# Soft mixture of experts on one core: weights of the next stage fetched in steps from float16 copies, transposed x kept in DRAM, a plain first block, and PSUM seeded by ScalarE

## The chip, the cores and the metric

The kernel runs on one core of one Trainium2 chip. The metric is the device time of one execution in microseconds; the kernel before takes 1645.31 us (median of three executions).

## The reference

Every token goes through all eight experts, and the results are summed with softmax weights of its eight router logits:

```python
probs = softmax(router_logits)                      # (16, 512, 8)
for e in range(8):                                  # x: (16, 512, 512)
    output += probs[:, :, e:e+1] * (x @ expert_weights[e])   # weights: (8, 512, 2048)
```

So it is one product of an 8192 x 4096 matrix (x scaled by each expert's probability, experts side by side) with a 4096 x 2048 matrix, all of it float32 outside the kernel. The kernel multiplies in float16 and accumulates in float32.

## The kernel before

The rows are cut into 32 blocks `h` of 256 (`HQ`), the inner dimension into the first four and the last four experts, the output columns into two halves of 1024. A Strassen-like scheme with seven products instead of eight runs over these halves, where even blocks `h` are the upper and odd ones the lower half of the rows. Four of the seven products are computed by `sub_product`, which splits each once more in the same way (seven products of 8 matmuls in place of eight). The other three are plain and belong to the last loop.

The program has five stages, and this text calls them A, B, C, D and main:

- A: `sub_product(0, P1, ...)`, the first four experts with the left columns. Its results go to DRAM (`kept[1]`).
- B: `sub_product(0, P2, ...)`, the last four experts with the left columns. It loads A's results (`from_kept(1, ...)`), adds them to its products on VectorE (`keep` with `v`), and writes a finished quarter of the output.
- C: `sub_product(1, PQ, ...)`, with differences of weights, into `kept[5]`.
- D: `sub_product(1, P2, ...)`, with other differences, into `kept[4]`.
- main: 16 pairs of blocks, two 128-row halves `u` each: 32 rounds. A round has six products of 16 matmuls (`s2` with `w6`, `s3` with `w7`, `s4` with `w3`, two column blocks each), adds `kept` 1, 4 and 5 on VectorE, and stores three quarters of the output.

In `sub_product` a step `d` takes two blocks `h`: it loads x and the probabilities, makes the seven scaled operands `z` (eight VectorE instructions of 128x2048 float16 for the products with the probabilities and for sums and differences), and runs 2 x 56 matmuls of 128x512. There are eight steps in a stage.

x is loaded anew in each stage: `load_x` casts 128 rows from float32 to float16 by a DMA on the GpSimd queue (line 101), then transposes them by a DMA on SyncE's queue (line 102). The probabilities are written once to DRAM (`p_dram`) and broadcast over the partitions by `load_p` (line 107).

Weights are tiles of 128 x 8 x 512 float16 (1 MB): two experts by 512 columns. `load_w` fills one with two casting DMAs on the GpSimd queue (line 122), 1 MB of float32 read by each. There are 12 such tiles in `wpool`. A stage uses seven: four quarters, of which one is overwritten in place, and three more that `inner_weights` makes by VectorE subtractions (`t1`, `t2`, `t4`). C's four quarters need four subtractions more and D's need twelve; eight tiles of D's intermediate results are stored to DRAM (`td`, line 236) and loaded in main as `w6` and `w7` (line 244). `w3` is cast from float32 again.

All VectorE additions go through the helper `tt` (line 69), all matmuls through `mm` (line 143). PSUM has eight banks of 128x512. Every engine and each DMA queue runs its instructions in an order that is written out when the program is built: a planner plays the program through, and it gives each engine the earliest instruction in program order that is ready by its own reckoning and for which a buffer is free. On the chip each engine then follows that order and waits at an instruction whose inputs are late, with all that stands behind it.

## Time and profile before

| | |
|---|---|
| three executions | 1644.45, 1645.31 and 1648.5 us; median 1645.31 us |
| the profiled execution | 1647.06 us, of which the span is 1645.3 us |
| TensorE matmuls | 1465.4 us busy (89%), 6656 matmuls |
| VectorE | 1070.4 us busy (65%), 1126 instructions |
| ScalarE | 115.2 us (7%) |
| GpSimd | 156.1 us (9%), 268 instructions, nearly all of them the issue of DMAs |
| HBM | 235.14 MB read, 126.03 MB written |
| mean granted TensorE clock | 0.958 of full |

Durations in the rows below come from the one profiled execution. A matmul's own duration overlaps with that of its neighbours, so how fast TensorE goes is read from the number of matmuls in a stretch. "Idle before, releaser" is how long the engine stood still ahead of an instruction, and what ended this.

### The profile page before, as it was taken

To read this page: it belongs to the slowest core of one execution; us is meant where nothing else is said; L and a number is where in the kernel's file an instruction comes from. 1 tells how busy PE (TensorE), PEld (TensorE's weight loads), DVE (VectorE), ACT (ScalarE), POOL (GpSimd) and SP (SyncE) were. 2 spreads that over 40 slices of the span, in tenths; PEclk is the share of its full clock that TensorE was granted. 3 is DMA by queue.
4 is the path that set the end of the run, shared out by engine and by line. 5 is a ranking of instruction groups with operands and counts; after the bars stand their busy time and mean duration, and the time that the engine had idled before them with its cause. 6 is when DMAs were issued, how large, how long until landed. Compare 5 with 4: busy or idle time off the path is not lost.

```text
span 1645.3 us, 17059 instructions
## 1 busy us (share of the span) xinstructions
PE 1465.4 (89%) x6656; PEld 656.7 (40%) x6656; DVE 1070.4 (65%) x1126; ACT 115.2 (7%) x196; POOL 156.1 (9%) x268
## 2 busy tenths in 40 slices
PE   1799993679999564899999979999999999999998
PEld 0344441234443221344444433444444444444444
DVE  3775672488876344856665657877777777777733
ACT  0111110000001010111111100000000000000000
POOL 2211020101011211000000010000000000000000
PEclk9899998889999787899999988999999999999999
DMA  9998669989899999668865499766676666665432
GB/s 177 182 230 186 148 149 243 218 208 227 220 209 231 265 236 184 161 148 219 224 149 150 136 272 246 223 200 208 201 205 204 206 202 205 202 204 195 165 150 104
DMA packets 243409, 324.58 MB, mean 197 GB/s; under 512 B 118272, under 2 KB 179712, under 8 KB 241280
## 3 DMA queue, kind: packets, MB, share of 16 engines
q1 hardware_dynamic: 177664, 260.56, 52.5%
q0 software_dynamic: 65664, 62.93, 25.4%
q8 instruction: 52, 0.85, 0.2%
q14 instruction: 29, 0.24, 0.1%
HBM read 235.14 MB, written 126.03 MB: 220 GB/s over the span
## 4 chain that ended last, share of the span: by engine, by line
PE 66%; DMA 9%; issue 2%; DVE 1%; POOL 0%; SPq 0%; ACT 0%; DVEq 0%; POOLq 0%; ACTq 0%
PE ps L143 66%; DMA w<-in_expert_weights_dram 5%; DMA xs<-in_x_dram 1%; DMA t<-w 1%; DMA xT<-xs 1%; DVE w L69 1%; POOL w L122 0%; DVE z L69 0%; DVE m L69 0%; SPq L102 0%; ACT r L183 0%; SPq L107 0%; SPq L202 0%; DVEq L69 0%; SPq L236 0%
## 5 line engine op out<-in xcount | busy, mean ns | idle before, releaser
L143 PE MATMUL ps<-w,z 128*128 128x512 f16 x6656 | 1465.4, 384 | 175.4 <-DVE z L69 77.6
L143 PEld LDWEIGHTS <-z 128*128 128x128 f16 x6656 | 656.7, 99 | 983.6 <-issue 136.5
L69 DVE TENSOR_TENSOR z<-xT,pT 128x2048 f16<-128x2048 f16 x256 | 308.8, 1218 | 28.4 <-DMA xT<-xs 13.4
L69 DVE TENSOR_TENSOR z<-z 128x2048 f16<-128x2048 f16 x224 | 272.6, 1219 | 18.5 <-PE ps L143 16.6
L69 DVE TENSOR_TENSOR m<-ps,m 128x512 f32<-128x512 f32 x192 | 130.6, 689 | 198.9 <-PE ps L143 190.3
L69 DVE TENSOR_TENSOR m<-ps,r 128x512 f32<-128x512 f32 x192 | 131.6, 687 | 134.4 <-PE ps L143 101.8
L101 POOL DMA_DIRECT2D xs<-in_x_dram x192 | 102.2, 534 | 1180.5 <-DMA xT<-xs 1161.3
L69 DVE TENSOR_TENSOR w<-w 128x4096 f16<-128x4096 f16 x32 | 73.1, 2288 | 151.1 <-DMA w<-in_expert_weights_dram 108.5
L183 ACT COPY r<-ps 128x512 f32<-128x512 f32 x192 | 112.6, 586 | 825.7 <-PE ps L143 726.4
L69 DVE TENSOR_TENSOR m<-m 128x1024 f32<-128x1024 f32 x96 | 114.4, 1219 | 0.3
L122 POOL DMA_DIRECT2D w<-in_expert_weights_dram x72 | 54.0, 760 | 145.7 <-DVE w L69 83.9
L69 DVE TENSOR_TENSOR r<-ps,m 128x512 f32<-128x512 f32 x64 | 43.6, 687 | 22.0 <-PE ps L143 16.9
L69 DVE TENSOR_TENSOR m<-r,ps 128x512 f32<-128x512 f32 x64 | 43.7, 682 | 9.8 <-PE ps L143 9.7
L80 DVE TENSOR_REDUCE mx<-lg 128x64 f32<-128x512 f32 x1 | 0.7, 686 | 6.9 <-DMA lg<-in_router_logits_dram 6.9
L82 ACT ACT_TABLE_LOAD x1 | 1.3, 1283 | 6.9 <-DMA lg<-in_router_logits_dram 6.9
L84 DVE TENSOR_REDUCE sm<-lg 128x64 f32<-128x512 f32 x1 | 0.7, 686 | 0.7 <-ACT lg L82 0.7
L89 ACT CAST ph<-pf 128x256 f16<-128x256 f32 x1 | 0.4, 404 | 10.0 <-DVE pf L69 10.0
L69 DVE TENSOR_TENSOR pf<-lg,sm 128x512 f32<-128x512 f32 x1 | 1.1, 1065 | 0.0
L69 DVE TENSOR_TENSOR lg<-lg,mx 128x512 f32<-128x512 f32 x1 | 0.7, 693 | 0.0
L82 ACT ACTIVATE lg<-lg 128x512 f32<-128x512 f32 x1 | 0.6, 630 | 0.2 <-DVE lg L69 0.2
L85 DVE RECIPROCAL sm<-sm 128x64 f32<-128x64 f32 x1 | 0.6, 553 | 0.0
L69 DVE TENSOR_TENSOR ph<-pf 128x256 f16<-128x256 f32 x1 | 0.4, 426 | 0.0
(5 smaller groups left out, 0.8 us busy)
## 6 DMA issues: line engine op xcount, KB each, us to landing
m<-kept SPq DMA_DIRECT2D x128, 512.0 KB, 5.3
out_dram<-m SPq DMA_DIRECT2D x128, 512.0 KB, 3.6
kept<-m SPq DMA_DIRECT2D x96, 512.0 KB, 4.1
w<-in_expert_weights_dram POOLq DMA_DIRECT2D x72, 512.0 KB, 13.5
pT<-p_dram SPq DMA_DIRECT2D x128, 256.0 KB, 4.4
xs<-in_x_dram POOLq DMA_DIRECT2D x192, 128.0 KB, 5.3
t<-w SPq DMA_DIRECT2D x8, 1024.0 KB, 7.6
w<-t SPq DMA_DIRECT2D x8, 1024.0 KB, 6.7
```

What stands on the lines that cost most here:

```text
L69: nc.vector.tensor_tensor(out=o, in0=a, in1=b, op=op)
L80: nc.vector.tensor_reduce(out=mx, in_=lg, axis=AX, op=mybir.AluOpType.max)
L82: nc.scalar.activation(out=lg, in_=lg, func=mybir.ActivationFunctionType.Exp)
L84: nc.vector.tensor_reduce(out=sm, in_=lg, axis=AX, op=ADD)
L85: nc.vector.reciprocal(out=sm, in_=sm)
L89: nc.scalar.copy(ph[:, 0:HE], pf[:, HE:E])
L101: nc.gpsimd.dma_start(out=xs, in_=x_f[ds(h * HQ + j * P, P), :])
L122: nc.gpsimd.dma_start(out=t[:, ds(e * C, C), :], in_=expert_weights[e0 + e, :, ds(n0, NB)].rearrange("(c p) n -> p c n", p=P))
L143: nc.tensor.matmul(ps, z, w, start=start, stop=stop, skip_group_check=True)
L183: nc.scalar.copy(r, ps)
```

## The change

- Weights: each 512-column block that is cast from float32 is stored once as float16 in DRAM (`raw`) by a DMA on the GpSimd queue; later uses load that copy (1 MB, one DMA, also GpSimd). Two sets of differences are stored likewise (`t1d`, `t2d`). The fetching, subtracting and storing for the next stage is a generator (`prep`) of which one step is taken in the program after each step `d` of the running stage.
- x: the first time that a block is used, `load_x` casts and transposes it and stores the result in DRAM (`x_dram`); later uses load this by one DMA on SyncE's queue.
- Start: step `d = 0` of stage A is computed plainly: 512 rows, 128 matmuls in place of 112, with operands that TensorE makes (16 matmuls of x by a diagonal matrix of probabilities, which transposes and scales at once; the results are copied out by ScalarE and VectorE). The 512 rows have a small softmax of their own. Eight matmuls of zeros open the eight PSUM banks.
- Stage B stores its results (`kept[2]`) and adds nothing; its evictions are copies on ScalarE as in the other stages. Main loads `kept[2]`, adds it to `kept[1]` on VectorE (128x1024) and stores that quarter of the output.
- main: ScalarE copies `kept[1]` into two PSUM banks, the products with `w6` accumulate on this, and the products with `w7` accumulate on the same two banks after VectorE has read them. Three VectorE additions of 128x1024 in a round are gone, one new one is there, and two more evictions of 128x512.
- Buffers: `xpool` 8 tiles in place of 9, `spool` 5 in place of 3.

The core of the diff:

```diff
+    with tc.tile_pool(name="psum0", bufs=1, space=bass.MemoryType.PSUM) as psum0:
+        ...
+        for i in range(8):
+            nc.tensor.matmul(every[:, i, :], zero[:, 0:P], zero, start=True, stop=True)
...
+    def fetch(q, k, n, keep=True):
+        t = new_w()
+        if (q, k, n) in raw:
+            nc.gpsimd.dma_start(out=t, in_=raw[q, k, n])
+        else:
+            cast_w(q, k, n, t)
+            if keep:
+                save(raw, (q, k, n), t)
+        return t
+    def save(where, key, t):
+        where[key] = dram.tile([P, K8, NB], f16, name="wd" + "_".join(map(str, key)))
+        nc.gpsimd.dma_start(out=where[key], in_=t)
...
+    for j in range(NF):
+        diag = rpool.tile([P, HE, P], f16, name="diag", tag="r")
+        tt(diag, ident..., ph0..., MUL)
+        for c in range(C):
+            ps = bank()
+            mm(ps, xs0[j][:, ds(c * P, P)], diag.rearrange("p e t -> p (e t)"), True, True)
+            (nc.scalar.copy if c % 2 else nc.vector.tensor_copy)(z[:, :, c, :], ps...)
...
+        if h in x_dram:
+            nc.sync.dma_start(out=xT, in_=x_dram[h])
+        else:
+            ... (cast and transpose as before)
+            nc.sync.dma_start(out=x_dram[h], in_=xT)
...
+    def sub_product(r, odd, first, w, prep, start=0, xs=None):
+        steps = prep()
+        for d in range(start, NI // 2):
...
+            next(steps, None)
...
+    def weights_of_t1():                       # made during B, for C
+        for kn in BLOCKS:
+            t = fetch(22, *kn)
+            if kn[0] == 1:
+                yield
+        b = {}
+        for kn in BLOCKS:
+            t = fetch(12, *kn)
+            b[kn] = fetch(11, *kn)
+            tt(b[kn], t, b[kn], SUB)
+            save(t1d, kn, b[kn])
+            yield
+        ready[5] = yield from inner_weights(b)
+    def weights_of_t4():                       # made during C, for D
+        for kn in BLOCKS:
+            t, t2 = fetch(22, *kn), load(t1d, kn)
+            tt(t2, t, t2, SUB)
+            save(t2d, kn, t2)
+            b[kn] = fetch(21, *kn)
+            tt(b[kn], t2, b[kn], SUB)
+            yield
+    def weights_of_main():                     # made during D
+        for kn in BLOCKS:
+            t = fetch(22, *kn)
+            w7[kn] = fetch(12, *kn)
+            tt(w7[kn], t, w7[kn], SUB)
+            yield
+        for kn in BLOCKS:
+            w6[kn] = load(t2d, kn)
+        for kn in BLOCKS:
+            w3[kn] = fetch(22, *kn)
...
+            m1, m2, m5, m4 = (from_kept(r, q, u) for r in (1, 2, 5, 4))
+            tt(m2, m1, m2, ADD)
+            to_out(0, 0, m2)
+            ps = [bank() for _ in range(2)]
             for n in range(2):
-                tt(m1[:, ts(n, NB)], prod(s2, w6, n), m1[:, ts(n, NB)], ADD)
+                nc.scalar.copy(ps[n], m1[:, ts(n, NB)])
+                prod(s2, w6, n, ps[n])
+                tt(m1[:, ts(n, NB)], ps[n], m5[:, ts(n, NB)], ADD)
             for n in range(2):
-                tt(u3[:, ts(n, NB)], prod(s3, w7, n), m1[:, ts(n, NB)], ADD)
-            tt(m4, u3, m4, SUB)
-            tt(m1, m1, m5, ADD)
-            tt(m5, u3, m5, ADD)
+                prod(s3, w7, n, ps[n])
+                tt(m5[:, ts(n, NB)], ps[n], m5[:, ts(n, NB)], ADD)
+                tt(m4[:, ts(n, NB)], ps[n], m4[:, ts(n, NB)], SUB)
```

## Rows read from the trace of the kernel before

**Rows 1.** Windows by stage; columns: stretch, length, engines' busy us (instructions), PEclk, DMA share, GB/s.
```profile
0.00:244.00 244.00, 197.99 (x896) 88.69 (x897) 148.59 (x150) 40.17 (x68) 43.43 (x76) 0.98 0.91 179
244.00:490.00 246.00, 195.93 (x883) 87.22 (x882) 164.81 (x196) 0.00 (x0) 26.80 (x46) 0.91 0.92 220
490.00:761.00 271.00, 205.18 (x892) 89.54 (x890) 151.37 (x146) 36.72 (x63) 37.97 (x61) 0.88 0.94 202
761.00:953.00 192.00, 192.00 (x892) 87.02 (x890) 124.66 (x136) 37.17 (x64) 13.80 (x26) 1.00 0.66 178
953.00:1641.00 688.00, 674.31 (x3101) 304.25 (x3099) 480.47 (x503) 1.17 (x2) 34.11 (x61) 0.99 0.66 199
1100.00:1200.00 100.00, 100.00 (x465) 45.40 (x464) 73.55 (x78) 0.00 (x0) 5.83 (x11) 1.00 0.66 197
1500.00:1600.00 100.00, 100.00 (x465) 45.32 (x464) 62.68 (x68) 0.00 (x0) 0.00 (x0) 1.00 0.44 160
```

**Rows 2.** Waits of the whole span: us in total, times, longest us.
```profile
DVE w L69 <- DMA w<-in_expert_weights_dram: 108.5, 11, 25.7
...
PE ps L143 <- DVE r L69: 50.1, 4, 24.5
```

**Rows 3.** Timeline, start of B: start us, duration, engine, line, instruction, idle before and releaser.
```profile
282.73 2.29 DVE L69 TENSOR_TENSOR w<-w 128x4096 f16<-128x4096 f16 x1 [22.95 <-DMA w<-in_expert_weights_dram]
...
287.47 26.92 PE L143 MATMUL ps<-w,z 128*128 128x512 f16 x112 [20.22 <-DVE r L69]
```

**Rows 4.** Windows: the first 170 us of C.
```profile
490.00:660.00 170.00, 107.31 (x449) 45.66 (x447) 81.83 (x74) 17.59 (x30) 29.48 (x45) 0.83 1.10 227
```

**Rows 5.** Timeline, the start of the program.
```profile
1.24 6.09 POOL L122 DMA_DIRECT2D w<-in_expert_weights_dram  x8 [0.80 <-POOLq L301]
...
15.88 0.75 POOL L122 DMA_DIRECT2D w<-in_expert_weights_dram  x1 [2.05 <-DMA w<-in_expert_weights_dram]
...
26.01 6.70 DVE L69 TENSOR_TENSOR w<-w 128x4096 f16<-128x4096 f16 x3 [6.56 <-DMA w<-in_expert_weights_dram]
26.62 2.67 SPq L102 DMA_TRANSPOSE xT<-xs  x2
...
35.86 5.58 PE L143 MATMUL ps<-w,z 128*128 128x512 f16 x16 [35.86 <-DVE z L69]
...
51.60 68.62 PE L143 MATMUL ps<-w,z 128*128 128x512 f16 x305 [10.15 <-DVE z L69]
```

**Rows 6.** Timeline, from D to main.
```profile
953.82 20.88 PE L143 MATMUL ps<-w,z 128*128 128x512 f16 x96
954.28 1.50 POOL L122 DMA_DIRECT2D w<-in_expert_weights_dram  x2 [31.15 <-PE ps L143]
...
982.67 1.87 PE L143 MATMUL ps<-w,z 128*128 128x512 f16 x4 [7.97 <-DMA w<-in_expert_weights_dram]
...
```

**Rows 7.** DMA queues of the whole span: packets, MB, share of 16 engines' time.
```profile
q1 hardware_dynamic: 177664, 260.56, 52.5%
q0 software_dynamic: 65664, 62.93, 25.4%
```

**Rows 8.** The page's groups: busy us, mean ns of one, idle before and releaser.
```profile
L69 DVE TENSOR_TENSOR z<-z 128x2048 f16<-128x2048 f16 x224 | 272.6, 1219 | 18.5 <-PE ps L143 16.6
L69 DVE TENSOR_TENSOR m<-ps,m 128x512 f32<-128x512 f32 x192 | 130.6, 689 | 198.9 <-PE ps L143 190.3
L183 ACT COPY r<-ps 128x512 f32<-128x512 f32 x192 | 112.6, 586 | 825.7 <-PE ps L143 726.4
L69 DVE TENSOR_TENSOR m<-m 128x1024 f32<-128x1024 f32 x96 | 114.4, 1219 | 0.3
```

**Rows 9.** DMA issues in the window 1000 to 1500 us (main): KB each, median us to landing.
```profile
m<-kept SPq DMA_DIRECT2D x72, 512.0 KB, 5.2
```

**Rows 10.** Timeline in main: a VectorE eviction and what it waited for.
```profile
1319.69 0.69 DVE L69 TENSOR_TENSOR m<-ps,m 128x512 f32<-128x512 f32 x1 [1.63 <-PE ps L143]
```

**Rows 11.** Instructions of tile w on the GpSimd queue: ns min/median/max, first and last start.
```profile
L122 POOL DMA_DIRECT2D w<-in_expert_weights_dram x72: 742/750/884, 1.2 to 960.2; - x72
```

More of the change, by code (lines that the diff above doesn't have):

```diff
@@ L66, with bank, mm, new_w @@
     psum = ctx.enter_context(tc.tile_pool(name="psum", bufs=8, space=bass.MemoryType.PSUM))
+    K8 = 2 * C
+    BLOCKS = ((0, 0), (1, 0), (0, 1), (1, 1))
     def tt(o, a, b, op):
         nc.vector.tensor_tensor(out=o, in0=a, in1=b, op=op)
+    def bank():
+        return psum.tile([P, NB], f32, name="ps", tag="ps")
+    def mm(ps, z, w, start, stop):
+        nc.tensor.matmul(ps, z, w, start=start, stop=stop, skip_group_check=True)
+    raw = {}
+    def new_w():
+        return wpool.tile([P, K8, NB], f16, name="w", tag="w")
@@ new lines, with cast_x @@
+    lg_f = router_logits.flatten_outer_dims()
+    P2, P1, PQ = 0, HE, 2 * HE
+    first = [0, P, 2 * HQ, 2 * HQ + P]
+    NF = len(first)
+    lg0 = rpool.tile([P, NF, E], f32, name="lg0", tag="r")
+    for j in range(0, NF, 2):
+        nc.sync.dma_start(out=lg0[:, ds(j, 2)], in_=lg_f[ds(first[j], 2 * P), :].rearrange("(j p) e -> p j e", p=P))
+    xs0 = []
+    def cast_x(row):
+        xs = spool.tile([P, H], f16, name="xs", tag="xs")
+        nc.gpsimd.dma_start(out=xs, in_=x_f[ds(row, P), :])
+        return xs
@@ new lines @@
+    ident = rpool.tile([P, P], f16, name="ident", tag="r")
+    nc.vector.memset(ident, 1.0)
+    nc.gpsimd.affine_select(out=ident, in_=ident, compare_op=mybir.AluOpType.is_equal, fill=0.0, base=0,
+                            pattern=[[-1, P]], channel_multiplier=1)
+    xs0.append(cast_x(first[0]))
+    b11 = {kn: new_w() for kn in BLOCKS}
+    cast_w(11, 0, 0, b11[0, 0])
+    for row in first[1:]:
+        xs0.append(cast_x(row))
+    cast_w(11, 1, 0, b11[1, 0])
+    cast_w(11, 0, 1, b11[0, 1])
@@ L186, in sub_product, with keep @@
-                r1 = keep(prod(1, "x"), 0, L)
+                        mm(banks[b], z[p][:, k, ds(u * P, P)], w[p][:, k, :], start and k == 0, k == K8 - 1)
+                    return banks[b]
+                def keep(ps):
+                    t = rpool.tile([P, NB], f32, name="r", tag="r")
+                    nc.scalar.copy(t, ps)
+                    return t
+                L, RR = slice(0, NB), slice(NB, NH)
+                o = [mpool.tile([P, NH], f32, name="m", tag="m") for t in range(2)]
@@ L238 @@
-    w = inner_weights(*q4)
-    sub_product(1, P2, w, to_kept(4), None)
-    def load_t(r, i):
-        t = wpool.tile([P, K8, NB], f16, name="w", tag="w")
-        nc.sync.dma_start(out=t, in_=td[r][i])
-        return t
-    w6 = [load_t(2, i) for i in range(4)]
-    w7 = [load_t(3, i) for i in range(4)]
-    w3 = [load_w(HE + 2 * k, NH + n * NB) for k, n in ((0, 0), (0, 1), (1, 0), (1, 1))]
+                to_kept(r, 2 * d + 1, u, o[1])
+            next(steps, None)
+        for _ in steps:
+            pass
@@ new lines, with weights_of_21 @@
+    ready = {}
+    def weights_of_21():
+        b = {}
+        for kn in BLOCKS:
+            b[kn] = fetch(21, *kn)
+            yield
+        ready[2] = yield from inner_weights(b)
+    o0 = [mpool.tile([P, NH], f32, name="m", tag="m") for _ in range(NF)]
+    for n in range(2):
+        ps = [bank() for _ in range(NF)]
+        for k in range(2):
+            for e in range(2):
+                for j in range(NF):
+                    for c in range(C):
+                        mm(ps[j], z0[j][:, (2 * k + e) * C + c, :], b11[k, n][:, e * C + c, :],
+                           k + e + c == 0, k + e == 2 and c == C - 1)
+        for j in range(NF):
+            nc.scalar.copy(o0[j][:, ts(n, NB)], ps[j])
@@ L252 @@
+    sub_product(4, 1, P2, ready[4], weights_of_main)
     for q in range(NI):
```

205 lines of the change are left out of this document (102 added, 103 removed).

## Prediction

> **What bounds the kernel now.** I first read the windows by stage [rows 1]. In main 465 matmuls pass in 100 us, 0.215 us each; the program's 6656 would take 1431 us at that pace, and the span is 1645.3 us, so 214 us are lost. The stages say where. A stage A to D has 896 matmuls, 192.6 us at full pace (some records are missing from the counts): A took 244 us, a loss of 51; B 246, a loss of 53; C 271, a loss of 78; D 192, none. Main's 3072 matmuls would take 660.5 us and took 688, a loss of 27.5; 4.5 us lie behind the last matmul. In main's steady part TensorE never stops, at the full clock (2.4 GHz), so only starts and changes of stage have something to give.
>
> Next, the waits [rows 2]: VectorE stood 108.5 us for weights from DRAM, in 11 waits, and TensorE stood for VectorE. The start of B shows the link [rows 3]: one subtraction of weights waits 22.95 us for its DMAs, and the evictions that stand behind it in VectorE's order come so late that TensorE stands 20.22 us. The order was written for transfers faster than those of the chip. In C the 16 engines' shares add up to 1.10 [rows 4]; shares add beyond 1 where queues overlap, so I read this as saturated. In those 170 us only 449 matmuls ran, 96.5 us of work: 73.5 of C's 78 us lie there.
>
> **Prices of transfers.** The queue rows [rows 7] give, per MB written: casting DMAs from GpSimd 0.254 x 1645.3 / 62.93 = 6.6 us of all engines, everything else 0.525 x 1645.3 / 260.56 = 3.3 us. C's chain of weights (16 tiles cast, 8 stored) is 16 x 6.6 + 8 x 3.3 = 132 us; beside it run x, probabilities and results.
>
> **C.** After the change the chain made during C (four steps of three loads and one store, all 1 MB float16) costs 16 x 3.3 = 53 us. With the loss in proportion, 78 x 53 / 132 = 31 us remain. Ends: 0 if the steps are spread over the 192 us, 60 if the twelve dependent transfers are slowed by latency. I take 31, because nothing in the trace makes the planner hold back: B's first weights were issued at 15.88 us [rows 5], 230 us before they were used, so a step in the program does not by itself delay its DMAs or the subtractions that VectorE then waits at. Gain 47.
>
> **B.** The chain for C's weights was 8 cast tiles, 53 us. It becomes 8 cast tiles, 12 stores and 4 loads: 53 + 53 = 106 us, twice as much, since the copies that C, D and main use are made here. Against this the rest gets lighter. Per step d there were 0.5 MB of x cast, 0.5 MB transposed, 0.5 MB of probabilities, 2 MB kept results loaded and 2 MB stored, 3.3 + 16.5 = 20 us; now 3 MB, 10 us. Eight steps and the chain are 186 us of 192.6: it fits if spread, barely. Placed early, as before, 106 + 2 x 10 us against the 40 us or so that the order will allow is a loss as large as before. Ends 0 and 75; I take 35. Gain 18. Taking the additions of kept results off VectorE costs nothing here: ScalarE copies 0.586 us [rows 8] and was idle in B.
>
> **D.** It had no loss. Now it fetches eight tiles and makes four subtractions at its beginning: 27 us of transfers, of which a part shows at VectorE. Ends 0 and 13 (half); I take 5.
>
> **Start of main.** The eight casting loads of `w3` were issued from 954.28 us, when D's tiles came free, and TensorE ran dry at 974.7 and waited for them until 996, 7.97 us ahead of the first of these matmuls [rows 6]. Now `w6` (three of four tiles) and `w3` are loaded, 7 x 3.3 = 23 us, the first tile 48 matmuls (10 us) before D ends; `w3` is wanted 64 matmuls (14 us) into main. These 24 us just cover it, but kept results and x share the engines. Ends 0 and 20; I take 8. Gain 20.
>
> **Start of the program.** Before [rows 5]: eight weight DMAs issued from 1.24 us, the last landed by about 26 us, some 3.1 us per DMA; x queued behind; first matmuls at 35.86, steady from 51.60 with 16 done. After: the same weights, with eight x tiles of a quarter of the bytes each in between (8 x 0.8 = 6 us), land by 32 us. The four x tiles and the first weights tile are 4 x 0.8 + 2 x 3.1 = 9.4 us of transfers, so landed by 11 us; 16 operand matmuls at the lower of the two clocks (1.2 GHz, 0.43 us each) are 7 us: plain work from about 18 us. The plain block's last 32 matmuls follow the last tile: done at 39 us at the earliest. Step d = 1 needs its x transposed and multiplied: 9 us from the first transpose (26.62) to the first matmul before, 25 to the steady pace; from 30 us this gives 39 to 55, middle 47. By then 112 of the old matmuls' worth is done, 24 us: a loss of 23, plus about 4 us of unsteady running. The extra matmuls (16 for operands, 16 of the plain block, 8 of zeros) lie in this time. Worse end: the in-place subtraction of A's weights must wait for the stores of their copies, 4 MB, which can stand behind B's eight casts: 32 + 25 + 13 = 70 us, a loss of 46. I take 30 of the range 15 to 46. Gain 21.
>
> **Main's rounds.** VectorE: seven `z` and one add of 128x1024 at 1.219, eight evictions at 0.689 [rows 8], 15.3 us of the round's 96 x 0.215 = 20.6 us; before, 16.3. DMA: 8 x 0.5 MB of kept and output per round in place of 6, but no casts and no transposes. The share was 0.66, and 0.44 where mostly kept and output run, at 160 GB/s [rows 1]; (153 x 8/6 + 37) = 241 GB/s at that price is 0.66 again. ScalarE's two seeds (1.2 us) wait for nothing but `kept[1]`, loaded a round ahead; nothing else stands in its order, so I cost them at zero (uncovered: one landing, 5.2 us [rows 9]). New is a tight link: the `w7` products accumulate on the banks that VectorE has just to read, so each read must be done within one product, 16 x 0.215 = 3.4 us, where before it had banks to spare. A read waits out at most one `z` (1.2) and takes 0.7: 1.5 us of slack. VectorE runs ahead of TensorE in main (it waited 1.63 us for a bank [rows 10]). The new add of `kept[2]` is not held by TensorE but by a landing, and can make VectorE wait in its order. Ends 0 and 2 us a round; I take 0.3, so 10 us.
>
> **The queue of GpSimd.** The stores and reloads of weights move from SyncE's queue to GpSimd's (16 before, 56 now), beside 96 casts. The rows show no price for this: an issue takes 0.75 us, at most 0.884, beside a VectorE that is busy most of the time [rows 11]. The Trainium skill (SBUF — State Buffer, sections "SBUF: two separate sides" and "Who interferes with whom") says that a DMA issued by GpSimd can't write its descriptors while VectorE runs an operation in a two-port mode, and advises the other queues; it counts copies and casts among these operations and doesn't name the kernel's subtractions. Were the subtractions among them, each of the 56 could be held by one.
>
> **The sum,** against the profiled execution (1647.06 us, of which 1.76 lie outside the span): 1431 + 30 (start) + 35 (B) + 31 (C) + 5 (D) + 8 (start of main) + 10 (rounds) + 4.5 (tail) + 1.8 = 1556. The median lies 1.75 us below the profiled execution: 1555.
>
> **Rivals.**
> 1. All steps are covered. B, C, D and main's rounds lose nothing, the start 25: 1431 + 25 + 5 + 4.5 + 1.8 = 1467, some 1470 to 1500. For it: DMA work per stage fits into each stage if spread, and the program is now ordered that way. Against: B fits by 6 us only, and the run-ahead at 15.88 us.
> 2. The chains show as before. The transfers are raw, but VectorE still waits at each: B 75, C 60, D 13, main's start 15, program's start 46, rounds 10: 1431 + 219 + 6.3 - 1.8 = 1655 at its very worst, 1600 to 1640 as I see it. For it: B's chain doubles.
> 3. Slower: TensorE waits in main's rounds. The place is VectorE's read of the two banks; the mechanism, that the add of `kept[2]` stands ahead of it and waits for a landing of 5.2 us [rows 9] instead of being ready. A read that is 5.2 us late exceeds the slack of 1.5 by 3.7 us; 32 rounds are 118 us: 1555 - 10 + 118 = 1663. It decides from 3.2 us a round on (100 / 32). Against: VectorE is idle for a quarter of each round [rows 1], and the loads have a round's time.
> 4. GpSimd's DMAs are held by VectorE. A subtraction takes 2.29 us [rows 3]; 56 issues held by it make 128 us of late weights, of which at worst all shows: 1683. Rows 11 speak against it: no issue was stretched by even 0.2 us. The Trainium skill's page behind it is the one named above (SBUF — State Buffer, same sections); nothing in this trace agrees with it so far.
>
> **How the numbers follow.** Forecast (1500 to 1600) 0.47; rival 1 0.26; rival 2 0.14; rival 3 0.10, half of it above the time before; rival 4 0.03. What a measurement of this kernel tells from no change is about 0.3%, 5 us. Slower by more: half of rival 3, rival 4 and the worst of rival 2, 0.09; within 0.3%: 0.04; faster: 0.87. The range takes in rival 1's time but its lowest end and rival 2's: 1475 to 1635; outside lie 0.07 below and 0.12 above.
>
> **What would show it.** Right: windows of B and C with 35 and 31 us less matmul work than their length, VectorE's largest waits on loads of weights from the copies and not on float32 casts; first steady matmuls of step d = 1 near 47 us; main at 465 matmuls in 100 us. Wrong: stages of 193 us each (rival 1); VectorE's waits on weights as long as 108 us (rival 2); fewer than 455 matmuls per 100 us in main, with VectorE named as the releaser (rival 3); GpSimd issues over 2 us (rival 4).

## The result, and the profile after

The changed kernel takes 1586.8 us (median of four executions, 1580.85 to 1598.33), against 1645.7 for the kernel before on the same chip: a ratio of 0.965, 95% interval 0.959 to 0.970. The forecast was 1555, in a range of 1475 to 1635. The profiled execution took 1587.45 us, with a span of 1585.8.

Windows of the changed kernel by stage (A, B, C, D, main, then steady parts of main), in the columns of [rows 1]:

```profile
0.00:244.00 244.00, 211.53 (x936) 93.11 (x937) 142.91 (x154) 45.05 (x77) 41.81 (x74) 0.95 0.96 221
244.00:475.00 231.00, 201.70 (x899) 89.63 (x898) 132.78 (x137) 37.52 (x64) 26.29 (x44) 0.92 0.84 237
475.00:692.00 217.00, 198.74 (x900) 88.55 (x898) 142.15 (x142) 37.52 (x64) 16.47 (x31) 0.96 0.77 216
692.00:899.00 207.00, 193.12 (x895) 87.49 (x894) 141.19 (x147) 37.95 (x65) 6.37 (x12) 0.97 0.54 198
899.00:1582.00 683.00, 668.49 (x3072) 300.88 (x3071) 430.73 (x489) 37.17 (x64) 0.00 (x0) 1.00 0.68 229
1300.00:1400.00 100.00, 98.08 (x453) 44.08 (x452) 70.95 (x80) 5.90 (x10) 0.00 (x0) 1.00 0.69 232
1400.00:1500.00 100.00, 96.69 (x447) 43.52 (x445) 64.73 (x74) 5.89 (x10) 0.00 (x0) 1.00 0.66 219
```

I use one measure for all kernels below: the time from the first matmul of a stage to the first of the next, less 0.215 us for each of its matmuls. For A it is the time at which B starts, less 192.6 us, so that the extra matmuls of the plain block count as lost. "To main" is D with the first two rounds of main, where the change of weights falls; "rounds" are the other thirty. Each row is from one profiled execution, the last column the median of all. In us:

| kernel | A | B | C | to main | rounds | median |
|---|---|---|---|---|---|---|
| before | 51.6 | 56.5 | 79.7 | 19.5 | 2.6 | 1645.3 |
| forecast | 30 | 35 | 31 | 13 | 10 | 1555 |
| changed | 51.5 | 38.1 | 24.0 | 17.6 | 18.5 | 1586.8 |
| e1, no plain block | 67.3 | 35.2 | 30.9 | 18.3 | 24.0 | 1603.6 |
| e2, probabilities stored by ScalarE's queue | 46.1 | 39.9 | 27.4 | 17.8 | 18.3 | 1584.6 |
| e3, all steps after the stage's loop | 73.8 | 38.9 | 22.9 | 17.3 | 17.3 | 1608.5 |
| e4, `kept[2]` added by GpSimd | 49.4 | 37.4 | 27.1 | 17.9 | 58.2 | 1627.7 |
| e5, subtractions held behind the matmul step | 48.6 | 0.7 | 0.7 | 18.7 | 13.4 | 1526.1 |
| e6, no float16 copies of weights | 47.5 | 26.4 | 35.9 | 55.8 | 23.2 | 1626.7 |
| e7, no copies of x | 48.6 | 56.1 | 27.6 | 32.7 | 56.9 | 1656.2 |
| e8, e5 with 11 operand, 9 kept slots | 49.8 | 0.7 | 6.9 | 21.0 | 50.3 | 1562.4 |
| e9, e5 with A's steps later, first round unseeded | 36.5 | 3.4 | 0.7 | 17.1 | 20.0 | 1516.4 |
| e10, e9 with 13 operand, 7 kept slots | 36.2 | 3.6 | 0.7 | 15.3 | 2.4 | 1495.6 |
| e11, e5 with banks of their own for `w7` | 49.7 | 0.7 | 0.7 | 17.4 | 14.8 | 1520.9 |
| e12, e5 with 11 operand slots | 47.1 | 0.7 | 8.2 | 21.4 | 55.5 | 1571.7 |

For the changed kernel 1431 + 51.5 + 38.1 + 24.0 + 17.6 + 18.5 and a tail of 5.2 give the span of 1585.9.

The row of the kernel before differs from the losses that the prediction reads from [rows 1]. Its windows were cut at round figures: the one for main holds 3101 matmuls, 29 more than main has, so 6 us of D were counted as main's loss. The first matmuls of B, C, D and main are at 244.2, 493.3, 765.6 and 959.0 us, and by these main's rounds lost only 2.6 us before the change. They lose 18.5 now.

A single stage varies between executions. C's program is the same in the changed kernel, e1, e2 and e4, and its loss is 24.0, 30.9, 27.4 and 27.1 us; the rounds of the changed kernel, e1 and e2 lose 18.5, 24.0 and 18.3. So differences of under some 7 us in one stage say little. The profile of e1 is the slowest of its four executions (1613.5 us), that of e5 the fastest (1519.8).

The waits of the changed kernel over the whole span, as in [rows 2]:

```profile
DVE m L84 <- DMA m<-kept: 194.6, 30, 8.8
...
DVE w L84 <- DMA w<-wd: 96.6, 11, 27.8
...
PE ps L90 <- ACT r L279: 59.7, 10, 14.3
...
DVE w L84 <- DMA w<-in_expert_weights_dram: 10.5, 2, 5.3
```

VectorE still waits 96.6 + 10.5 us for weights, against 108.5 [rows 2]; the loads are now those of the float16 copies. Through ScalarE's evictions this reaches TensorE, at a lower price than before: B and C together lose 62 us where they lost 136. No run separates why an equal wait costs less. The timeline at the start of B, in the place of [rows 3]:

```profile
298.17 2.29 DVE L84 TENSOR_TENSOR w<-w 128x4096 f16<-128x4096 f16 x1 [27.77 <-DMA w<-wd]
...
301.79 8.50 PE L90 MATMUL ps<-w,z 128*128 128x512 f16 x27 [14.34 <-ACT r L279]
```

One subtraction holds VectorE for 27.77 us, and with it the operations behind it that feed the evictions; TensorE stands for 14.34.

The start of the program, where [rows 5] stood:

```profile
16.92 27.79 PE L90 MATMUL ps<-w,z 128*128 128x512 f16 x128
...
27.45 0.40 ACT L204 CAST ph<-pf 128x256 f16<-128x256 f32 x1 [7.89 <-DVE pf L84]
...
43.48 0.37 SPq L222 DMA_DIRECT2D x<-xT  x1
...
43.95 2.82 SPq L208 DMA_DIRECT2D p_dram<-ph  x4
...
55.36 2.36 DVE L84 TENSOR_TENSOR z<-xT,pT 128x2048 f16<-128x2048 f16 x2 [17.67 <-DMA pT<-p_dram]
...
56.65 5.83 PE L90 MATMUL ps<-w,z 128*128 128x512 f16 x16 [11.93 <-DVE z L84]
...
92.38 7.84 PE L90 MATMUL ps<-w,z 128*128 128x512 f16 x29 [10.48 <-ACT r L279]
```

The plain block runs from 16.92 to 44.7 us at the full clock. The next step waits for its probabilities: they are ready in SBUF at about 28 us, but their stores to DRAM stand in SyncE's queue behind the store of a transposed x, which goes out at 43.48 when its transposes have landed, and are issued at 43.95 us.

Windows of the changed kernel over most of A, in the columns of [rows 1]:

```profile
0.00:50.00 50.00, 38.22 (x152) 15.66 (x152) 20.62 (x29) 12.23 (x21) 16.18 (x30) 0.97 1.11 237
50.00:100.00 50.00, 30.97 (x125) 12.99 (x126) 24.70 (x23) 5.27 (x9) 9.41 (x16) 0.79 1.07 227
100.00:150.00 50.00, 48.33 (x224) 21.82 (x223) 39.98 (x43) 9.38 (x16) 7.92 (x15) 1.00 1.11 249
150.00:200.00 50.00, 50.00 (x233) 22.70 (x232) 30.68 (x34) 9.38 (x16) 5.30 (x10) 1.00 1.04 265
```

A loses 26 us in its first 50 us (24 of the 152 matmuls there are operands and zeros, and 16 more the plain block's surplus), 23 in the next 50, and under 2 from 100 to 200 us, although the DMA share is as high there (1.11 and 1.04).

From D to main, where [rows 6] stood:

```profile
875.05 0.53 POOL L122 DMA_DIRECT2D w<-wd  x1 [153.93 <-PE ps L90]
...
885.41 0.53 POOL L109 DMA_DIRECT2D w<-wd  x1 [1.20 <-PE ps L90]
...
887.10 0.42 SPq L244 DMA_DIRECT2D m<-kept  x1
...
898.57 1.11 ACT L409 COPY ps<-m 128x512 f32<-128x512 f32 x2 [14.56 <-DMA m<-kept]
899.21 31.12 PE L90 MATMUL ps<-w,z 128*128 128x512 f16 x132 [14.10 <-ACT ps L409]
```

Here TensorE waits for ScalarE's seed (its copy of `kept[1]` into PSUM), which waits for `kept[1]`. That load is issued on SyncE's queue at 887.10, some 2 us after GpSimd's queue has issued seven loads of weights of 1 MB each, and the seed starts 11 us later.

In main's steady part, start of a round:

```profile
1213.35 1.23 DVE L84 TENSOR_TENSOR m<-m 128x1024 f32<-128x1024 f32 x1 [8.42 <-DMA m<-kept]
...
1215.63 2.48 DVE L84 TENSOR_TENSOR m<-ps,m 128x512 f32<-128x512 f32 x4
...
1226.00 20.88 PE L90 MATMUL ps<-w,z 128*128 128x512 f16 x96 [1.15 <-DVE m L84]
```

The add of `kept[2]` waits 8.42 us for its landing; four evictions come right behind it, in one run, and the rest of the round is late by 1.15 us.

### The profile page after: what moved, and what is told of

Its sections match the earlier page's. It is cut to its first block, busy times and chain, and to the rows that moved or that the text cites. A ratio compares the mean times of both kernels' runs of the same rounds, so it can differ in the third digit from the quotient of the medians.

```text
span 1585.8 us, 16968 instructions
## 1 busy us (share of the span) xinstructions
PE 1473.6 (93%) x6696; PEld 659.7 (42%) x6696; DVE 989.8 (62%) x1066; ACT 195.2 (12%) x333; POOL 90.9 (6%) x161
## 4 chain that ended last, share of the span: by engine, by line
PE 47%; DMA 34%; DVE 11%; issue 5%; SPq 1%; POOL 1%; ACT 0%; DVEq 0%; POOLq 0%; ACTq 0%
PE ps L90 47%; DMA out_dram<-m 14%; DMA w<-in_expert_weights_dram 6%; DVE z L84 6%; DMA m<-kept 5%; DVE m L84 5%; DMA xT<-xs 3%; DMA w<-wd 2%; DMA xT<-x 1%; DMA pT<-p_dram 1%; DMA wd<-w 1%; DMA xs<-in_x_dram 1%; SPq L244 0%; POOL w L101 0%; DMA p_dram<-ph 0%
## 5 line engine op out<-in xcount | busy, mean ns | idle before, releaser
L279 ACT COPY r<-ps 128x512 f32<-128x512 f32 x248 | 145.4, 586 | 693.3 <-PE ps L90 592.4
L84 DVE TENSOR_TENSOR m<-ps,m 128x512 f32<-128x512 f32 x256 | 165.3, 683 | 55.1 <-PE ps L90 54.9
L84 DVE TENSOR_TENSOR m<-m 128x1024 f32<-128x1024 f32 x32 | 39.2, 1225 | 194.6 <-DMA m<-kept 194.6
L84 DVE TENSOR_TENSOR w<-w 128x4096 f16<-128x4096 f16 x32 | 73.2, 2289 | 113.7 <-DMA w<-wd 96.6
L409 ACT COPY ps<-m 128x512 f32<-128x512 f32 x64 | 37.6, 590 | 616.1 <-DVE m L84 586.5
L162 POOL DMA_DIRECT2D xs<-in_x_dram x68 | 36.4, 540 | 270.7 <-DMA xT<-xs 264.3
L101 POOL DMA_DIRECT2D w<-in_expert_weights_dram x32 | 24.3, 768 | 56.9 <-PE ps L90 52.0
L109 POOL DMA_DIRECT2D w<-wd x24 | 12.9, 536 | 166.3 <-PE ps L90 119.8
L118 POOL DMA_DIRECT2D wd<-w x24 | 13.1, 546 | 126.2 <-DMA w<-in_expert_weights_dram 61.4
L122 POOL DMA_DIRECT2D w<-wd x8 | 4.3, 532 | 174.5 <-PE ps L90 157.5
L90 PE MATMUL ps<-diag,xs 128*128 128x512 f16 x16 | 7.0, 619 | 5.2 <-DMA xs<-in_x_dram 5.2
L190 DVE CAST z<-ps 128x512 f16<-128x512 f32 x8 | 5.5, 692 | 3.2 <-PE ps L90 3.2
## 6 DMA issues: line engine op xcount, KB each, us to landing
w<-wd POOLq DMA_DIRECT2D x32, 1024.0 KB, 10.1
```

What stands on the lines that cost most here:

```text
L84: nc.vector.tensor_tensor(out=o, in0=a, in1=b, op=op)
L90: nc.tensor.matmul(ps, z, w, start=start, stop=stop, skip_group_check=True)
L101: nc.gpsimd.dma_start(out=t[:, ds(e * C, C), :], in_=expert_weights[(q // 10 - 1) * HE + 2 * k + e, :, ds((q % 10 - 1) * NH + n * NB, NB)] ...
L109: nc.gpsimd.dma_start(out=t, in_=raw[q, k, n])
L118: nc.gpsimd.dma_start(out=where[key], in_=t)
L122: nc.gpsimd.dma_start(out=t, in_=where[key])
```

## The experiments

My theory after the result: B and C lose because VectorE reaches the subtractions of weights before their loads land, as it did before; A loses through the place of the probabilities' stores in SyncE's queue; main's rounds through the add of `kept[2]`. The rivals were that DMA bandwidth sets B and C, the x copies A, and the link of the shared banks main.

**e1: no plain block.** A starts with step `d = 0` as the others do.

```diff
-    first = [0, P, 2 * HQ, 2 * HQ + P]
...
-    o0 = [mpool.tile([P, NH], f32, name="m", tag="m") for _ in range(NF)]
...
-    sub_product(1, 0, P1, w, weights_of_21, start=1, xs=xs1)
+    sub_product(1, 0, P1, w, weights_of_21)
```

> The changed kernel without the plain first block and without operands made by TensorE: stage A runs all eight steps d = 0 to 7 as sub_product does, the weights of A being cast first as in the kernel before. Everything else as in the changed kernel (1586.8 us). In its trace stage A loses 51 us, as much as before the change, though 112 matmuls' worth are done by 44.6 us. Theory (the plain block does its part, some 20 us, and what follows it, a late start of step d = 1 and full DMA engines until 100 us, takes it back; these stay without it): 1597 to 1610 us, stage A's loss 62 to 75 us. Rival (stage A is bound by its DMAs whatever TensorE does first): 1580 to 1592 us, loss 45 to 56 us.

Measured: 1603.6 us, ratio 0.974 (0.967 to 0.980). The first product comes at 48.4 us, and A loses 67.3. The plain block is worth 15.8 us in A (16.8 by the medians of the whole); without it the changed A is 16 us worse than the one before (51.6). The total and the loss of A are in the ranges of the theory.

**e2: the stores of the probabilities on ScalarE's queue.**

```diff
-        nc.sync.dma_start(out=p_dram[:, :, ds(r * J, J)], in_=ph[ds(r * NHQ, NHQ)])
+        nc.scalar.dma_start(out=p_dram[:, :, ds(r * J, J)], in_=ph[ds(r * NHQ, NHQ)])
```

> The changed kernel with one edit: the four stores of the probabilities are issued from ScalarE's queue and not from SyncE's. In the trace of the changed kernel they were ready at 28.2 us and issued at 43.95 us, behind a store of transposed x that waited on SyncE's queue; TensorE then stood 12.3 us at 44.3 us. Theory (a queue order, not bandwidth): the hole of 12.3 us falls under 4 us and the total by 6 to 14 us, 1573 to 1581. Rival (the DMA engines are full in this stretch, so an earlier store only moves the hole): the sum of TensorE's idle time from 44 to 120 us stays at 29 us or more and the total within 1583 to 1591.

Measured: 1584.6 us, 0.962 (0.959 to 0.966). The hole behind the plain block only shrinks from 11.9 to 10.1 us, and the total is in the range of the rival. (The 29 us of idle time in what I expected were too high: the four longest stands from 44 to 120 us are 26.0 us in the changed kernel and 21.9 here.) The stores now go out from 28.0 us on, 16 earlier, but the load that reads them back is issued at 49.77 (52.10 in the changed kernel). Transfers of e2 from 25 to 56 us: the share of GpSimd's DMAs, then the stores of the probabilities with KB each and median us to landing:

```profile
q0 software_dynamic: 3164, 6.72, 81.9%
...
p_dram<-ph ACTq DMA_DIRECT2D x4, 48.0 KB, 16.5
```

Stores of 48 KB take 16.5 us to land (6.5 in the changed kernel), beside weights and x cast by GpSimd's DMAs, which have 82% of the engines. The queue was not what held the step for the most part; that full engines did is argued from this share. The Trainium skill (DMA: Bandwidth & Descriptors, "Issuing engines are not separate DMA queues") says that another issuing engine saves only the time of the issue, since all transfers share the 16 engines; these 16.5 us agree.

**e3: all steps of the fetch after the stage's loop in the program.**

```diff
                 to_kept(r, 2 * d + 1, u, o[1])
-            next(steps, None)
         for _ in steps:
```

> The changed kernel with all steps of the generators taken after a stage's loop instead of one after each step d, so the next stage's weights stand in the program behind the whole stage. Nothing else differs. The changed kernel loses 38 us in B and 24 us in C. Theory (the planner issues whatever is ready and has a buffer, so the place of a step in the program hardly moves it): B 30 to 46 us, C 16 to 32 us, total 1575 to 1600 us. Rival (the steps do space the transfers): B over 55 or C over 45 us, total over 1610 us.

Measured: 1608.5 us, 0.976 (0.973 to 0.978). B and C stay as they were, 38.9 and 22.9: their steps do nothing to hold the work back, since the planner takes what it reckons ready. In A the loss grows to 73.8, which I hadn't expected and which takes the total out of the theory's range; a subtraction waits 24.66 us for cast weights there and TensorE stands 20.04 behind it.

**e4: `kept[2]` added on GpSimd.**

```diff
-            tt(m2, m1, m2, ADD)
+            nc.gpsimd.tensor_tensor(out=m2, in0=m1, in1=m2, op=ADD)
```

> The changed kernel with the addition of kept 2 in main's rounds on GpSimd instead of VectorE. In the trace of the changed kernel VectorE waits there 195 us in 30 rounds for the load, and main's rounds lose 18.5 us from 943 us on. Theory (VectorE's wait for a landing delays the reads of the two banks, which TensorE waits for): main's rounds lose under 6 us, total 1570 to 1578. Rival (GpSimd's 128x1024 addition holds up VectorE, or the reads are late for another reason): main's rounds lose 15 us or more, total 1583 or more.

Measured: 1627.7 us, 0.989 (0.986 to 0.992); main's rounds lose 58.2 instead of 18.5. VectorE indeed no longer waits for `kept`, but the wait doesn't vanish. Waits of e4:

```profile
ACT ps L409 <- DMA m<-kept: 534.4, 26, 23.9
POOL m L405 <- DMA m<-kept: 454.6, 24, 22.5
```

The changed kernel's seeds waited 29.6 us for `kept[1]`; here 534.4. A GpSimd add takes 2.35 us (1.225 on VectorE). My theory fell: the total is in the range of the rival. With the add on GpSimd the loads land later for those who need them; whether that is because the slots of `kept` come free later, the run doesn't separate.

**e5: the subtractions of each step of the fetch stand on VectorE's queue behind the last eviction of its matmul step.** The loads are not held.

```diff
-                tt(o[1][:, L], r3, prod(4, "d"), SUB)
+                last = tt(o[1][:, L], r3, prod(4, "d"), SUB)
                 to_kept(r, 2 * d + 1, u, o[1])
-            next(steps, None)
+            with tc.issue_after(last.ins):
+                next(steps, None)
```

> The changed kernel with one edit of order: the subtractions of weights of each step of the generator are placed on VectorE's queue behind the last eviction of the step d after which they stand in the program; their DMAs stay as early as they are. In the trace of the changed kernel B loses 38 us and C 24 us. Theory (the transfers fit into the stage, only VectorE stands at them too early): B and C lose under 8 us each, total 1527 to 1545. Rival (the volume of the transfers is the limit, B's chain doubled): B loses 25 us or more, total over 1565.

Measured: 1526.1 us, 0.926 (0.923 to 0.930). Windows of e5, B and C, then its wait for the weights' copies:

```profile
241.00:434.00 193.00, 193.00 (x896) 87.54 (x895) 132.01 (x137) 37.55 (x64) 24.32 (x41) 1.00 0.96 275
434.00:628.00 194.00, 194.00 (x901) 87.91 (x899) 143.97 (x141) 37.55 (x64) 18.32 (x35) 1.00 0.82 249
```
```profile
DVE w L84 <- DMA w<-wd: 11.0, 3, 6.7
```

B and C lose 0.7 us each. The loads were not moved back: the first load of a copy is issued at 283.1 us, 286.9 in the changed kernel. B's share of the DMA engines rises to 0.96 and still all is covered. The transfers fit. What cost 38 and 24 us was VectorE arriving at the subtractions before the loads had landed.

**e6: weights cast from float32 at each use.**

```diff
-        if (q, k, n) in raw:
-            nc.gpsimd.dma_start(out=t, in_=raw[q, k, n])
-        else:
-            cast_w(q, k, n, t)
...
+        cast_w(q, k, n, t)
```

> The changed kernel without the float16 copies of weights: every fetch casts from float32 again, nothing of the four weight quadrants is stored, and the early fetch of the last quadrant in B, which only served its copy, is gone. The stored differences stay. Made during B: 8 casts and 4 stores, 66 us of transfers instead of 106; during C: 8 casts, 4 loads, 4 stores, 79 us instead of 53; during D: 8 casts instead of 8 loads; main's last four tiles are cast. Theory (a stage's loss follows its own chain): B's loss falls from 38 to 15 to 30 us, C's rises from 24 to 38 to 60, start of main from 18 to 22 to 35, total 1590 to 1625. Rival (what the copies save and what they cost in B cancel): 1580 to 1590.

Measured: 1626.7 us, 0.988 (0.986 to 0.989). B is lighter by 12 us without the stores and reloads, C heavier by 12, and the way to main loses 55.8 in place of 17.6. That is where the copies earn most. I had expected less there (22 to 35), more in C (38 to 60), and a total of at most 1625.

**e7: x cast and transposed in each stage, as before.**

```diff
-            x_dram[h] = dram.tile([P, C, HQ], f16, name=f"x_{h}")
-            nc.sync.dma_start(out=x_dram[h], in_=xT)
```

> The changed kernel without x kept in DRAM: every use casts and transposes x again. Theory (B is where the engines are full; 64 casts and 64 transposes in B and as many in D): A loses 8 to 15 us less than now (51), because no stores of x stand on SyncE's queue; B loses 50 to 80 us (38 now); D and main have room and change by under 10 us; total 1595 to 1630. Rival (x is off the path): B 30 to 46 us, total 1570 to 1590.

Measured: 1656.2 us, 1.005 (1.002 to 1.007): all of the gain is gone. B loses 56.1 as expected (it makes 32 casts and 32 transposes of x, not the 64 that I wrote). A, at 48.6, is no better than in e4 and e5 (49.4 and 48.6), which keep the stores of x, so these aren't what loads A. Main's rounds lose 56.9, against my expectation of hardly a change, and the total is 26 us over my range. I read this as the loads of `kept` sharing the engines with the casts and transposes of x, which the kernel before, with three loads a round, bore at a loss of 2.6 us; no run shows it.

The parts don't add: without the plain block, the copies of weights or those of x the kernel is 17, 40 or 69 us slower, 126 in all, and the change gains 59.

**e8: e5 with nine slots for kept results and eleven for operands** (a slot of either kind takes 4 KB per partition, so one is traded for the other).

```diff
-    zpool = ctx.enter_context(tc.tile_pool(name="zpool", bufs=12))
+    zpool = ctx.enter_context(tc.tile_pool(name="zpool", bufs=11))
...
-    mpool = ctx.enter_context(tc.tile_pool(name="mpool", bufs=8))
+    mpool = ctx.enter_context(tc.tile_pool(name="mpool", bufs=9))
```

> The kernel with the subtractions behind their step (1526.1 us), and the pool of kept and output tiles with 9 slots instead of 8, the pool of operands with 11 instead of 12. In main SyncE waits at loads of kept results for a slot, that is for an earlier store's landing: 275.5 us in 93 waits between 1000 and 1500 us of the changed kernel. Theory (too few slots make the kept loads late, VectorE waits at its addition, the reads of the two banks are late): main's rounds lose 0 to 7 us instead of 13.4, total 1511 to 1522. Rival (the loads are late for the order of SyncE's queue, or one operand slot less costs as much): main's rounds lose 11 us or more, total 1522 to 1535.

Measured: 1562.4 us, 0.948 (0.946 to 0.950). The rounds lose 50.3, not 0 to 7, and the total is above the rival's range too. Waits of e8 in main (890 to 1480 us):

```profile
DVE m L84 <- DMA m<-kept: 63.9, 22, 6.6
...
PE ps L90 <- DVE m L84: 32.2, 12, 4.5
```

A third of the wait for `kept` is left, and yet TensorE waits longer for VectorE. The slot taken from the operands was the suspect; e12 tries it alone.

**e9: e5, with B's weights fetched two steps later in A and behind the casts of x, and main's first round without its seed** (on VectorE `kept[1]` is added to `kept[5]` and subtracted from `kept[4]` instead).

```diff
         b = {}
+        yield
+        yield
         for kn in BLOCKS:
             b[kn] = fetch(21, *kn)
...
-            with tc.issue_after(last.ins):
+            with tc.issue_after(last.ins), (tc.issue_after(cast_x.last.ins) if r == 1 else nullcontext()):
                 next(steps, None)
...
+            if q == u == 0:
+                tt(m5, m1, m5, ADD)
+                tt(m4, m4, m1, SUB)
```

> The kernel with the subtractions behind their step (1526.1 us), with two edits in places that don't touch each other. First, in stage A the casts of B's weights start two steps later and stand on GpSimd's queue behind the casts of x of their step; there A lost 38.6 us (10.1, 13.0 and 15.5 us in its three parts). Second, main's first round is not seeded (kept 1 is added on VectorE instead), as TensorE stood 15.2 us there for ScalarE's copy of a late kept tile. Theory: in A B's casts and their stores hold up x and the probabilities, the third part falls from 15.5 to under 8 us; the start of main (15.7 and 3.0 us) to under 8 us in all; total 1500 to 1515. Rival for A (x is late for the order of SyncE's queue): its third part stays over 12 us. Rival for main (operands or weights are late by as much): over 13 us stay.

Measured: 1516.4 us, 0.922 (0.921 to 0.924). A's loss falls from 48.6 to 36.5, of which B gives back 3. The total is just above the expected range. In A the engines are as full as in the changed kernel, and yet 186 matmuls pass from 50 to 100 us where 125 did; window of e9:

```profile
50.00:100.00 50.00, 44.51 (x186) 19.16 (x187) 36.63 (x37) 7.62 (x13) 9.95 (x18) 0.88 1.11 239
```

The start of main keeps its loss, only a little later, as the rival said; timeline of e9:

```profile
822.25 1.89 PE L90 MATMUL ps<-w,z 128*128 128x512 f16 x8 [1.51 <-DMA w<-wd]
...
832.18 2.52 DVE L84 TENSOR_TENSOR m<-m 128x1024 f32<-128x1024 f32 x2 [9.06 <-DMA m<-kept]
...
836.81 1.44 PE L90 MATMUL ps<-w,z 128*128 128x512 f16 x3 [8.86 <-ACT ps L419]
```

TensorE begins, waits for the weights of `w6` themselves, then for `kept`. The seed is only the first place where the burst of loads shows.

**e11: e5, with the `w7` products in banks of their own**, two more additions of 128x1024 a round, as a test of the shared banks.

```diff
+            tt(m4, m5, m4, ADD)
             ps = [bank() for _ in range(2)]
...
+            tt(m4, m1, m4, SUB)
             for n in range(2):
-                prod(s3, w7, n, ps[n])
-                tt(m5[:, ts(n, NB)], ps[n], m5[:, ts(n, NB)], ADD)
-                tt(m4[:, ts(n, NB)], ps[n], m4[:, ts(n, NB)], SUB)
+                p7 = prod(s3, w7, n)
+                tt(m5[:, ts(n, NB)], p7, m1[:, ts(n, NB)], ADD)
+                tt(m4[:, ts(n, NB)], p7, m4[:, ts(n, NB)], ADD)
```

> The kernel with the subtractions behind their step (1526.1 us, of which main's rounds lose 13.4), with banks of their own for the products with w7, so TensorE no longer waits for VectorE to have read two banks; VectorE has two more additions of 128x1024 in a round (17.7 us of 20.6). Theory (main's loss is that link): main's rounds lose under 6 us, total 1515 to 1522. Rival (VectorE is late itself, by its waits for kept tiles; the link only shows it): main's rounds lose 13 us or more, and more with the extra additions, total 1526 to 1560.

Measured: 1520.9 us, 0.926 (0.923 to 0.928): the total is in the theory's range, but the rounds, 14.8 against 13.4 in e5, are in the rival's. Waits of e11 from 950 to 1480 us:

```profile
PE ps L90 <- DVE m L84: 10.2, 10, 1.8
```

In e5 these waits are 9.3 us in 10, with the shared banks. The extra additions load VectorE, so this isn't the link alone, but the wait stays as it was without the link. The medians differ by 5 us, but the executions overlap. So the shared banks aren't most of main's loss.

**e12: e5 with eleven operand slots, all else as in e5.**

```diff
-    zpool = ctx.enter_context(tc.tile_pool(name="zpool", bufs=12))
+    zpool = ctx.enter_context(tc.tile_pool(name="zpool", bufs=11))
```

> The kernel with the subtractions behind their step (1526.1 us; main's rounds lose 13.4) and 11 slots for operands instead of 12, with the 8 slots for kept and output tiles as they were. With 9 of these and 11 operand slots main's rounds lost 50.3 us. Theory (an operand slot less is what cost: VectorE can no longer prepare operands far enough ahead to absorb its waits): main's rounds lose 40 us or more, total 1550 to 1565. Rival (the ninth slot for kept tiles changed the order for the worse): main's rounds lose 8 to 25 us, total 1520 to 1538.

Measured: 1571.7 us, 0.956 (0.953 to 0.959); rounds 55.5. One operand slot less costs 42 us in main, which explains e8; the total is even above the theory's range.

**e10: e9 with thirteen operand slots and seven for kept results.**

```diff
-    zpool = ctx.enter_context(tc.tile_pool(name="zpool", bufs=12))
+    zpool = ctx.enter_context(tc.tile_pool(name="zpool", bufs=13))
...
-    mpool = ctx.enter_context(tc.tile_pool(name="mpool", bufs=8))
+    mpool = ctx.enter_context(tc.tile_pool(name="mpool", bufs=7))
```

> The kernel of the run with A's later steps moved and the first main round unseeded (1516.4 us, main's rounds 20.0 us beyond full pace), but 13 operand slots (z) and 7 slots for kept results (m), the mirror of the run with 11 and 9. Theory: main's rounds hang on how far VectorE runs ahead with operands, so one operand slot more gives back what one less cost in part: main's rounds below 10 us, total 1500 to 1508. Rival: both kinds are needed by VectorE's order as it stands, and a kept slot less delays the loads of kept results, on which the add of kept[2] and the seeds wait: main's rounds above 40 us, total 1537 or more. Between (10 to 40 us): neither decides.

Measured: 1495.6 us, 0.907 (0.905 to 0.908), the fastest of all, below the theory's range; the rounds, 2.4, are in it. First the 400 us from 1000 on in the changed kernel, then in e12, then in e10; last, from 880 to 1480 us, e5's wait of VectorE for `kept`, then e10's waits for TensorE and for `kept`:

```profile
1000.00:1400.00 400.00, 390.44 (x1802) 176.04 (x1801) 267.89 (x302) 22.42 (x38) 0.00 (x0) 1.00 0.69 231
```
```profile
1000.00:1400.00 400.00, 370.78 (x1672) 165.34 (x1670) 245.88 (x278) 20.07 (x34) 0.00 (x0) 0.98 0.66 219
```
```profile
1000.00:1400.00 400.00, 400.00 (x1855) 181.34 (x1854) 281.52 (x309) 22.99 (x39) 0.00 (x0) 1.00 0.70 237
```
```profile
DVE m L84 <- DMA m<-kept: 183.4, 28, 8.4
```
```profile
DVE m L84 <- PE ps L90: 187.9, 133, 2.8
...
DVE m L84 <- DMA m<-kept: 5.1, 8, 1.2
```

TensorE never stops in e10's steady main. VectorE waits there for TensorE's products and hardly any more for `kept`: 5.1 us, where e5 has 183.4. So e10 doesn't absorb the old waits by a longer lead; its order is another one, in which the add of `kept[2]` comes when its load has landed.

With eleven operand slots the rounds lose 50 to 56 us, with twelve 13 to 20 (e5, e9, e11), with thirteen 2.4. From twelve to eleven the operand slot alone was changed (e12); the ninth kept slot moved this by 5 (e8 against e12), within the spread. From twelve to thirteen a kept slot was taken away as well, so what each did in e10 is not separated.

## Why the prediction came out as it did

The size of the gain, 59 us, was forecast as 90. On the profiled execution 31 us are missing, and by the table they are A +21.5, B +3, C -7, the way to main +5, the rounds +8.5.

Against the kernel before, by the same measure, A gains nothing (21 forecast), B 18 (18), C 56 (47), the way to main 2 (15 for D and main's start together), and the rounds lose 16 (10).

- **What bounds the kernel, B and C: right, and shown.** B was forecast at 35 and measured 38.1, C at 31 and 24.0. The reason was that nothing makes the planner hold the subtractions back, so that VectorE waits for transfers which would fit. e3 shows that the place of the steps does nothing in B and C, and e5 that holding them back takes the whole loss away. The arithmetic of the transfers holds too: I had 186 us of DMA work for B; 0.84 x 231 = 194 us is what the window shows, 0.96 x 193 = 185 in e5. Rival 1, with all steps covered, is what e5 makes of these two stages, not what the change did. Rival 2's sign did come, VectorE's waits for weights of 107 us, but not its losses. The sizes are in part luck: B's 35 was chosen between ends of 0 and 75 without a sum; C's was scaled by its chain of transfers, and e6 agrees with such a scaling (a chain of 79 us in place of 53 loses 35.9 in place of 24.0), although e5 shows that the transfers as such cost B and C nothing.
- **Start of the program: the term that was mis-sized,** 30 forecast, 51.5 measured, so the gain of 21 is none. Plain work from 18 us was right (16.92); its end was 44.7, not 39. The step that failed is the next one: step `d = 1` at 47 us with "about 4 us of unsteady running" behind it. It came at 56.65, outside its range of 39 to 55; the transposes and the probabilities that it needs go through engines filled by casting loads, as I read e2, and I had spaced them as in the kernel before. The running part lost another 18.9. For that part I never made the sum of transfers that I made for B and C. The row was there: A's share in [rows 1] is 0.91 over 244 us, 222 us of the engines' time for 192.6 us of matmuls, and the change adds stores to A; now the share is 0.96, 234 us. But the sum alone doesn't decide: from 100 to 200 us TensorE loses under 2 us at a share of 1.11 and 1.04, so it is rather their order in the first 100 us that costs. e9 shows this for a part: B's weights fetched later within A return 12 us at as high a share. Of e9's remaining 36.5 us some 26 lie in its first 50 us, as in the changed kernel. The plain block does its work (15.8 us, e1), and the rest of the change takes it back. The worse end, an in-place subtraction that waits for the store of its copy, did not come: it ended by 37.7 us.
- **D and the start of main: near in size (13, measured 17.6), by another link than I named.** I counted the seven loads of weights against the matmuls that cover them, and named `kept` and x as sharing the engines. The weights didn't show first: `kept[1]`, behind them, did, by the seed that I had costed at zero, as waiting for a tile "loaded a round ahead". There is no round ahead at the start. e9 shows that without the first seed the burst shows in the weights and in the next `kept`.
- **Main's rounds: 10 forecast, 18.5 measured.** In the kernel before they lost 2.6, so the new main is 16 us slower there; no run puts the additions back into B to price that. The mechanism of rival 3 is there: the add of `kept[2]` holds VectorE for 6.6 us a time (185.5 us in 28 waits from 950 to 1580 us), and at most some 0.6 us a round reaches TensorE, in place of the 3.7 of that rival. Its sign came too: the 465 matmuls in 100 us that I asked for became 453 and 447, under its 455, with VectorE as the releaser (13.1 us in 14 waits). What I had wrong is the slack, which I put at 1.5 us of bank time. e12 shows that an operand slot is worth 42 us here; that VectorE's lead by such slots is what takes up the rest of the wait is argued, not shown.
- **Rival 4 did not come.** Issues of the stores and reloads of weights in the changed kernel; columns: ns min/median/max, first and last start:

```profile
L118 POOL DMA_DIRECT2D wd<-w x24: 534/547/557, 21.1 to 548.6; - x24
L109 POOL DMA_DIRECT2D w<-wd x24: 531/531/571, 286.9 to 885.4; - x24
```

No issue is stretched beside a VectorE that is busy 62% of the time. The Trainium skill (SBUF — State Buffer, "Who interferes with whom") says further, which my prediction left out, that operations on two tensors, as the subtractions are, have no two-port mode and were not seen to stall DMAs; this trace agrees.

So the total lies in the range because B and C, the largest terms, were near in size, and because the range of 160 us was wide beside the terms that missed by 21 and 8 us.

## What to carry to other kernels

Make the sum of transfers for each stage from the share in its window, also for the one where the change seems only to add a head start, and look at which transfers stand ahead of those that the next matmuls need: A gained nothing until transfers that were needed later were moved back within it (12 us). When an order written ahead lets an in-order engine reach an operation before its load, hold that operation behind the work that covers the load (61 us here from three lines) before moving or shrinking the transfers. When a new wait enters a steady loop, try the number of operand slots; here one slot of 4 KB per partition less cost some 42 us, and one more, in place of a kept slot, gave some 18 back.

## What the runs showed of the hardware

Landing times did not go by the size written. Issues of the changed kernel from 0 to 244 us, with KB each and median us to landing:

```profile
kept<-m SPq DMA_DIRECT2D x31, 512.0 KB, 4.8
w<-in_expert_weights_dram POOLq DMA_DIRECT2D x20, 512.0 KB, 12.2
wd<-w POOLq DMA_DIRECT2D x8, 1024.0 KB, 11.2
```

In the same stage a casting load that writes 0.5 MB (and reads 1 MB) takes two and a half times as long to land as a plain store of 0.5 MB, and as long as a plain store of 1 MB. The first and the last two use different queues, and no run separates this from the cast. Nor does a small transfer land sooner where others fill the engines: 48 KB took 16.5 us in e2, in some 400 packets each.

A stall also costs more than its own time. In the changed B the granted clock is 0.92, in e5's B, where TensorE never stood still, 1.00. A window of the changed kernel behind the stall of 14.34 us, in the columns of [rows 1]:

```profile
301.80:306.00 4.20, 4.20 (x10) 1.42 (x10) 4.20 (x7) 0.59 (x1) 0.00 (x0) 0.50 1.16 156
```

The clock is at the lower of its two levels (1.2 GHz), and ten matmuls take 4.2 us in place of 2.15; so some of B's loss is slower running and not standing.
